# Weights split into two parts by two GpSimd-queue DMAs and a ScalarE negation, in a four-layer block on one Trainium2 core

## The chip, the core and the metric

The kernel runs on one core of one Trainium2 chip. The metric is device time in microseconds (us), as the median of three runs. The engines are TensorE (PE in the profile, PEld for its weight loads), VectorE (DVE), ScalarE (ACT), GpSimd (POOL) and SyncE (SP); SP, ACT and POOL can also issue DMAs, which all run on the core's 16 DMA engines.

## The reference

512 tokens of 1024 features in fp32 pass through four mixers with a residual each, and a norm at the end:

```
h = rms_norm(x) * (1 + scale) + shift          # scale, shift, gate = silu(c) @ ada_w[l] + ada_b[l]
x = x + gate * ([conv31(h @ Wa) | rwkv7(h @ Wb)] @ even_w_out)     # layer 0
x = x + gate * ((topk_attention(h @ odd_w_in) * silu(g)) @ odd_w_out)  # layer 1
x = x + (lru(conv4(h @ lru_w_in)) * gelu(gate)) @ lru_w_out         # layer 2, width 1536
x = x + (forgetting_attention(h @ fox_w) * silu(g)) @ fox_w_out     # layer 3, 16 heads of 64
out = rms_norm(x, final_g)
```

What matters here: every `@` with a weight matrix is an fp32 product, and the result is compared at fp32 accuracy.

## The kernel before

Activations lie with the features in the partitions: eight tiles of 128 features by 512 tokens. TensorE takes operands of type fp32r, which carry fewer bits than fp32. So each fp32 operand is written as the sum of two fp32r tiles, a first part h and a remainder l, and each product is three matmuls (`mm3`, lines 161 to 165): first weight part times first activation part (L163), first weight part times the remainder of the activations (L164), and the remainder of the weights times the first activation part (L165).

Weights are used once, in column tiles of [128 partitions, up to 8 row tiles, 128], 512 KB each, 384 KB for `lru_w_out`, and 256 KB where a product is taken in halves. `wsplit` (line 126) prepares one of them:

- SP issues a DMA of the raw weights into a tile `wr` of a ring of three (L133);
- ScalarE casts each half of it to fp32r, `wh` (L138);
- GpSimd subtracts, `wl = wr - wh`, for each half (L139). `wh` and `wl` are rings of four half tiles, that is two whole weight tiles.

`wrows` (line 143) does the same for the first eight loads, which hold one row tile of seven column tiles each: DMA L148, cast L153, subtraction L154. Callers are `project`, `fill`, `lead`, `project_halves` and `project_tok`; the last passes a tag (`pT`) for the last weights of the kernel, so that these stand in another ring.

Each engine runs its own instructions in order. The order is set when the kernel is built: a list scheduler places the instructions of all engines by its own model, with priorities, and tiles are handed out from rings, so that an instruction waits until the last user of its buffer is done. A DMA is issued by its queue's engine in that same order: what stands behind a waiting instruction waits too.

Other work that the prediction names: the convolution's 27 multiply-adds for each of eight channel tiles on DVE (L835), with L840 on POOL; the recurrence's L622, L626 and L628; the softmax scaling by rows on POOL (L1235, L1487); and L1088, two DMAs that POOL issues, of 64 partitions by 512 fp32 from SBUF to SBUF.

## Time and profile before

| | |
|---|---|
| runs | 1833.74, 1839.56, 1842.38 us; median 1839.56 |
| profiled execution, first to last instruction | 1835.4 us (no device time of its own is given for it) |
| PE | 1685.5 us busy, 92% |
| DVE | 1319.1 us busy, 72% |
| ACT | 899.9 us busy, 49% |
| POOL | 866.9 us busy, 47% |
| granted TensorE clock, mean | 0.955 |
| DMA | 182.15 MB, mean 99 GB/s |

The page gives busy time by engine, the chain of work that ended last, and groups of instructions by line. A matmul's busy time in it overlaps that of the next, so a busy PE is not a PE at its peak; the distance between the starts of two matmuls is the better measure. Waits are put down to what released them last.

### The profile page before, as it was taken

What the parts mean: (1) busy time and instruction counts of PE and PEld (TensorE: products, weight loads), DVE (VectorE), ACT (ScalarE), POOL (GpSimd) and SP (SyncE); (2) the same over time, 40 slices, a digit from 0 to 9 for tenths busy, and PEclk for the clock granted to TensorE, in tenths of its full rate; (3) what the DMA queues carried; (4) which work ended last, traced back from release to release, by engine and by line L of the source; (5) the groups of instructions that cost most, each with busy time, mean ns of one, the idle gap of its engine ahead of it and who ended that gap; (6) DMA issues with size and microseconds to landing.
All of it is one profiled execution on the core that took longest, in us unless ns stands there. A gap on an engine that the chain in (4) does not pass through costs nothing.

```text
span 1835.4 us, 25614 instructions
## 1 busy us (share of the span) xinstructions
PE 1685.5 (92%) x9250; PEld 1311.0 (71%) x9250; DVE 1319.1 (72%) x2246; ACT 899.9 (49%) x1699; POOL 866.9 (47%) x682
## 2 busy tenths in 40 slices
PE   3997889999895999898999999999988899999998
PEld 2765678776664777765778788888766687776776
DVE  6689997897969786568969978734898721455552
ACT  2443234334333524466344677644767633555564
POOL 4555564444585422354435555344544443444343
PEclk9997898998988889999999999999999999999999
DMA  9412352214243852331225310022222233321211
GB/s 271 131 58 69 118 144 72 83 47 135 78 126 120 266 185 97 97 99 58 92 86 169 119 53 13 24 92 92 81 89 66 78 103 108 104 81 61 81 55 70
DMA packets 111055, 182.15 MB, mean 99 GB/s; under 512 B 37296, under 2 KB 57136, under 8 KB 110928
## 3 DMA queue, kind: packets, MB, share of 16 engines
q1 hardware_dynamic: 106736, 172.91, 30.1%
q10 hardware_dynamic: 4032, 7.34, 1.1%
q8 instruction: 73, 1.20, 0.3%
q14 instruction: 54, 0.44, 0.1%
q0 software_dynamic: 160, 0.26, 0.1%
HBM read 162.10 MB, written 18.12 MB: 98 GB/s over the span
## 4 chain that ended last, share of the span: by engine, by line
PE 58%; DVE 32%; ACT 4%; issue 4%; DMA 2%; SPq 0%; POOL 0%; DVEq 0%; ACTq 0%
PE ps L163 15%; PE ps L164 15%; PE ps L165 14%; DVE x L835 7%; DVE q L665 2%; DVE xc L1300 2%; DVE q L666 2%; PE ps L1494 1%; DVE SAV L438 1%; DVE u L1369 1%; PE ps L706 1%; PE ps L1477 1%; PE ps L1490 1%; PE ps L1238 1%; PE ps L538 1%
## 5 line engine op out<-in xcount | busy, mean ns | idle before, releaser
L139 POOL TENSOR_TENSOR wl<-wr,wh 128x512 fp32r<-128x512 f32 (+1 forms) x400 | 563.6, 1413 | 657.1 <-ACT wh L138 614.3
L163 PE MATMUL ps<-h,wh 128*128 128x512 f32 x1240 | 511.2, 416 | 31.2 <-DVE s L516 13.2
L165 PE MATMUL ps<-h,wl 128*128 128x512 f32 x1240 | 505.7, 408 | 6.0 <-POOL wl L139 6.0
L164 PE MATMUL ps<-h,wh 128*128 128x512 f32 x1240 | 506.2, 408 | 3.2 <-DVE h L328 2.7
L138 ACT CAST wh<-wr 128x512 fp32r<-128x512 f32 (+1 forms) x400 | 242.0, 609 | 409.4 <-PE ps L164 332.4
L163 PEld LDWEIGHTS ps<-h,wh 128*128 128x128 f32 x1240 | 244.5, 197 | 98.8 <-DVE s L516 17.0
L165 PEld LDWEIGHTS ps<-h,wl 128*128 128x128 f32 x1240 | 243.5, 196 | 63.0 <-POOL wl L139 7.1
L164 PEld LDWEIGHTS ps<-h,wh 128*128 128x128 f32 x1240 | 244.0, 197 | 57.2 <-issue 3.6
L835 DVE SCALAR_TENSOR_TENSOR x<-cu,vec,x 128x512 f32<-128x512 f32 x216 | 214.5, 995 | 4.7
L1235 POOL TENSOR_SCALAR pp<-pp,st 128x512 f32<-128x512 f32 x32 | 52.3, 1634 | 51.9 <-DVE st L1231 38.3
L1484 DVE CUSTOM_DVE_ANT_0 pp<-ps,nb 128x128 f32<-128x128 f32 (+3 forms) x64 | 30.8, 488 | 42.4 <-PE ps L1479 31.2
L1230 ACT ACTIVATE pp<-pp,st 128x512 f32<-128x512 f32 x64 | 46.3, 723 | 23.8 <-DVE st L1229 23.6
L665 DVE TENSOR_TENSOR q<-q,q 128x112 f32<-128x112 f32 (+25 forms) x108 | 46.1, 461 | 15.0 <-POOL q L657 11.7
L1487 POOL TENSOR_SCALAR pp<-pp,st 128x128 f32<-128x128 f32 (+1 forms) x32 | 31.4, 986 | 47.9 <-DVE st L1486 47.8
L1229 DVE CUSTOM_DVE_ANT_0 pp<-ps,bias 128x512 f32<-128x512 f32 x64 | 43.4, 679 | 6.2 <-PE ps L1238 4.2
L164 PE MATMUL ps<-wl,h 128*128 128x512 f32 x120 | 47.2, 393 | 0.0
L1485 ACT ACTIVATE pp<-pp,st 128x128 f32<-128x128 f32 (+3 forms) x64 | 35.9, 561 | 21.8 <-DVE st L1484 21.3
L163 PE MATMUL ps<-wh,h 128*128 128x512 f32 x120 | 46.5, 403 | 0.0
L165 PE MATMUL ps<-wh,h 128*128 128x512 f32 x120 | 46.5, 393 | 0.0
L1491 ACT COPY pT<-ps 128x128 f32<-128x128 f32 (+3 forms) x64 | 26.6, 423 | 39.6 <-PE ps L1490 38.8
L284 DVE TENSOR_TENSOR pT<-ps,pT 128x512 fp32r<-128x512 f32 x64 | 43.4, 680 | 2.3 <-ACT pT L283 2.1
L283 ACT CAST pT<-ps 128x512 fp32r<-128x512 f32 x64 | 36.6, 577 | 16.2 <-PE ps L1238 15.7
(522 smaller groups left out, 3480.7 us busy)
## 6 DMA issues: line engine op xcount, KB each, us to landing
wr<-in_even_w_in SPq DMA_DIRECT2D x50, 512.0 KB, 3.5
wr<-in_odd_w_in SPq DMA_DIRECT2D x39, 512.0 KB, 3.5
wr<-in_lru_w_in SPq DMA_DIRECT2D x24, 512.0 KB, 3.4
wr<-in_fox_w_qkg SPq DMA_DIRECT2D x24, 512.0 KB, 3.5
k<-in_ada_w SPq DMA_DIRECT2D x32, 256.0 KB, 3.0
wr<-in_odd_w_out SPq DMA_DIRECT2D x16, 512.0 KB, 3.8
wr<-in_lru_w_out SPq DMA_DIRECT2D x16, 384.0 KB, 3.1
AR<-in_ada_w SPq DMA_DIRECT2D x4, 1024.0 KB, 9.8
```

The costliest lines, as they stand in the source:

```text
L138: nc.scalar.copy(h[:, :n], raw[:, k:k + n])
L139: nc.gpsimd.tensor_tensor(out=l[:, :n], in0=raw[:, k:k + n], in1=h[:, :n].bitcast(F), op=OP.subtract)
L163: mm(ps, lhsT=w[0], rhs=x[0], start=first, stop=False)
L164: mm(ps, lhsT=w[0], rhs=x[1], start=False, stop=False)
L165: self.last_mm = mm(ps, lhsT=w[1], rhs=x[0], start=False, stop=last).ins
L284: nc.vector.tensor_tensor(out=l, in0=src, in1=h.bitcast(F), op=OP.subtract)
L665: eng.tensor_tensor(out=z, in0=Yu[:, a, b:b + 1].to_broadcast(sh), in1=Nu[:, b:b + 1, b + 1:].to_broadcast(sh), op=OP.mult)
L666: eng.tensor_tensor(out=Yu[:, a, b + 1:], in0=Yu[:, a, b + 1:], in1=z, op=OP.add)
L835: nc.vector.scalar_tensor_tensor(out=acc, in0=u[:, q:q + S], scalar=w[q], in1=acc, op0=OP.mult, op1=OP.add)
L1229: nc.vector.tensor_tensor_reduce(out=pp, in0=lg, in1=bias[t], scale=1.0, scalar=3e38, op0=OP.add, op1=OP.min, accum_out=mx)
L1230: nc.scalar.activation(pp, pp, AF.Exp, scale=-1.0, bias=mx, accum_out=sm)
L1235: (nc.vector if t % 2 else nc.gpsimd).tensor_scalar(out=pp, in0=pp, scalar1=sm, scalar2=None, op0=OP.mult)
```

## The change

A new helper `wparts` takes the place of load, cast and subtraction. A DMA issued by POOL writes the weights into the fp32r tile `h`, rounding on the way; ScalarE writes `l = -h`; a second POOL DMA reads the same weights from HBM again and adds them to `l` in place. There is no `wr` ring any more; `wh` and `wl` become rings of three whole tiles. (Comments and docstrings are dropped too, so lines move up by up to four: L1088 becomes L1084.)

```diff
     def wsplit(self, key, idx, k0, kn, rows=True, tag=None):
...
-        raw = self.wp.tile([P, 8, P], F, name=self.name("wr"), tag="wr", bufs=3)
-        nc.sync.dma_start(out=raw[:, :kn], in_=self.ins[key][idx][:, k0:k0 + kn])
-        out = []
-        n = kn if kn <= 4 else kn // 2
-        for k in range(0, kn, n):
-            h, l = (self.t(tag, (P, 4, P), R) if tag else self.wp.tile([P, 4, P], R, name=self.name(z), tag=z, bufs=4) for z in ("wh", "wl"))
-            nc.scalar.copy(h[:, :n], raw[:, k:k + n])
-            nc.gpsimd.tensor_tensor(out=l[:, :n], in0=raw[:, k:k + n], in1=h[:, :n].bitcast(F), op=OP.subtract)
...
+        h, l = self.wparts(self.ins[key][idx][:, k0:k0 + kn], kn, tag)
...
+    def wparts(self, src, n, tag=None):
+
+        nc = self.nc
+        h, l = ((self.t(tag, (P, 8, P), R) if tag else self.wp.tile([P, 8, P], R, name=self.name(z), tag=z, bufs=3))[:, :n] for z in ("wh", "wl"))
+        nc.gpsimd.dma_start(out=h, in_=src)
+        nc.scalar.mul(l, h.bitcast(F), -1.0)
+        nc.gpsimd.dma_start(out=l, in_=src, accum_op=OP.add)
+        return h, l
 
     def wrows(self, key, ct, k):
...
-        nc.sync.dma_start(out=raw[:, :n], in_=self.ins[key][ct[0]:ct[-1] + 1:d, :, k].rearrange("c p n -> p c n"))
...
+        h, l = self.wparts(self.ins[key][ct[0]:ct[-1] + 1:d, :, k].rearrange("c p n -> p c n"), n)
+        return [(h[:, i], l[:, i]) for i in range(n)]
```

In the built program POOL then issues 217 first-part DMAs (L142) and 217 adding DMAs (L144), ScalarE 217 negations (L143), and SP none of the weight loads. In POOL's order, 159 of the 217 pairs have no other first-part DMA between their two; for 59 pairs the two follow each other directly. The names are tiles: `wh` and `wl` the two parts, `wr` the raw weights, `in_...` a weight matrix in HBM, `pp` a block of softmax numerators, `V` values by tokens.

POOL, the values' projection at the start of the last layer, before:

```order
L139 TENSOR_TENSOR wl_13447<-wr_13444,wh_13446 128x512
L139 TENSOR_TENSOR wl_13451<-wr_13444,wh_13450 128x512
L139 TENSOR_TENSOR wl_13516<-wr_13513,wh_13515 128x512
L139 TENSOR_TENSOR wl_13520<-wr_13513,wh_13519 128x512
L139 TENSOR_TENSOR wl_13550<-wr_13547,wh_13549 128x512
L139 TENSOR_TENSOR wl_13554<-wr_13547,wh_13553 128x512
```

and the same place as changed:

```order
L142 DMA wh_12608<-in_fox_w_v 128x1024
L144 DMA wl_12609<-in_fox_w_v 128x1024
L142 DMA wh_12672<-in_fox_w_v 128x1024
L144 DMA wl_12673<-in_fox_w_v 128x1024
L142 DMA wh_12701<-in_fox_w_v 128x1024
L144 DMA wl_12702<-in_fox_w_v 128x1024
```

Six subtractions became three pairs of DMAs; the load of a weight tile now stands behind the adding DMA of the tile before it.

ACT at that place, before:

```order
L138 CAST wh_13446<-wr_13444 128x512
L138 CAST wh_13450<-wr_13444 128x512
L1408 COPY rb_13320<-ps_13407 128x512
L138 CAST wh_13515<-wr_13513 128x512
L138 CAST wh_13519<-wr_13513 128x512
L1401 ACTIVATE V_13316<-ps_13321,col_13368 128x512
```

and as changed:

```order
L143 ACTIVATE wl_12609<-wh_12608 128x1024
L1404 COPY rb_12499<-ps_12576 128x512
L143 ACTIVATE wl_12673<-wh_12672 128x1024
L1397 ACTIVATE V_12495<-ps_12500,col_12542 128x512
L1397 ACTIVATE V_12496<-ps_12501,col_12542 128x512
L143 ACTIVATE wl_12702<-wh_12701 128x1024
```

Two casts became one negation of twice the size, which stands ahead of the same evacuations of PSUM and waits for a DMA that POOL issues.

POOL in the attention of layer 1, as changed; the scalings L1231 (L1235 before) now stand among the DMA pairs:

```order
L142 DMA wh_9557<-in_odd_w_in 128x1024
L1231 TENSOR_SCALAR pp_8264<-pp_8264,st_8266 128x512
L144 DMA wl_9558<-in_odd_w_in 128x1024
L142 DMA wh_9703<-in_odd_w_in 128x1024
L1231 TENSOR_SCALAR pp_8302<-pp_8302,st_8304 128x512
L1060 TENSOR_TENSOR s_8915<-s_8915,tab_6271 128x512
L144 DMA wl_9704<-in_odd_w_in 128x1024
L1231 TENSOR_SCALAR pp_8379<-pp_8379,st_8381 128x512
```

A scaling behind an L144 waits until that DMA has been issued.

## Rows read from the trace of the kernel before

**Rows 1.** The page, the chain that ended last: shares of the span by engine, by line.

```profile
PE 58%; DVE 32%; ACT 4%; issue 4%; DMA 2%; SPq 0%; POOL 0%; DVEq 0%; ACTq 0%
PE ps L163 15%; PE ps L164 15%; PE ps L165 14%; DVE x L835 7%; DVE q L665 2%; DVE xc L1300 2%; DVE q L666 2%; PE ps L1494 1%; DVE SAV L438 1%; DVE u L1369 1%; PE ps L706 1%; PE ps L1477 1%; PE ps L1490 1%; PE ps L1238 1%; PE ps L538 1%
```

**Rows 2.** The page's costliest groups: busy us, mean ns, idle before, releaser.

```profile
L139 POOL TENSOR_TENSOR wl<-wr,wh 128x512 fp32r<-128x512 f32 (+1 forms) x400 | 563.6, 1413 | 657.1 <-ACT wh L138 614.3
L138 ACT CAST wh<-wr 128x512 fp32r<-128x512 f32 (+1 forms) x400 | 242.0, 609 | 409.4 <-PE ps L164 332.4
L835 DVE SCALAR_TENSOR_TENSOR x<-cu,vec,x 128x512 f32<-128x512 f32 x216 | 214.5, 995 | 4.7
```

**Rows 3.** Timeline of PE at full pace: start, us, engine, line, operation.

```profile
98.54 0.39 PE L163 MATMUL ps<-h,wh 128*128 128x512 f32 x1
...
99.22 0.39 PE L163 MATMUL ps<-h,wh 128*128 128x512 f32 x1
```

**Rows 4.** Line 835 (DVE): duration in ns, min/median/max, first and last start.

```profile
L835 DVE SCALAR_TENSOR_TENSOR x<-cu,vec,x x216: 721/752/1826, 83.0 to 516.6; 128x512 f32<-128x512 f32 x108
```

**Rows 5.** Timeline of DVE and of POOL around 178 us.

```profile
178.48 1.83 DVE L835 SCALAR_TENSOR_TENSOR x<-cu,vec,x 128x512 f32<-128x512 f32 x1
180.83 0.74 DVE L628 SCALAR_TENSOR_TENSOR s<-s,vec,s 128x512 f32<-128x512 f32 x1
...
178.47 1.29 POOL L139 TENSOR_TENSOR wl<-wr,wh 128x512 fp32r<-128x512 f32 x1 [0.46 <-ACT wh L138]
```

**Rows 6.** The chain in order of time: first and last of its stretched DVE pieces.

```profile
21.09 1.65 DVE SAV L438
...
1449.77 1.93 DVE u L1369
```

**Rows 7.** The page's DMA issues: count, KB each, median us from issue to landing.

```profile
wr<-in_odd_w_in SPq DMA_DIRECT2D x39, 512.0 KB, 3.5
wr<-in_lru_w_out SPq DMA_DIRECT2D x16, 384.0 KB, 3.1
AR<-in_ada_w SPq DMA_DIRECT2D x4, 1024.0 KB, 9.8
wr<-in_even_w_out SPq DMA_DIRECT2D x16, 256.0 KB, 2.7
```

**Rows 8.** Line 1088, POOL's own DMAs: issue ns min/median/max; landing.

```profile
L1088 POOL DMA_DIRECT2D ki<-ki x2: 517/632/747, 805.7 to 806.9; - x2
DMA to landing us min/median/max: 2.2/2.3/2.4
```

**Rows 9.** Timeline of ACT around 96 us: a weight tile's two casts, merged.

```profile
96.29 1.13 ACT L138 CAST wh<-wr 128x512 fp32r<-128x512 f32 x2
```

**Rows 10.** Line 133, the weight loads by matrix: issue ns, first and last start.

```profile
L133 SPq DMA_DIRECT2D wr<-in_odd_w_in x39: 327/328/425, 760.4 to 1032.4; - x39
L133 SPq DMA_DIRECT2D wr<-in_lru_w_in x24: 327/328/328, 1238.1 to 1400.6; - x24
L133 SPq DMA_DIRECT2D wr<-in_fox_w_qkg x24: 327/328/384, 1532.5 to 1726.7; - x24
L133 SPq DMA_DIRECT2D wr<-in_lru_w_out x16: 327/328/328, 1408.2 to 1485.8; - x16
L133 SPq DMA_DIRECT2D wr<-in_fox_w_v x8: 327/328/375, 1490.0 to 1527.1; - x8
```

**Rows 11.** Line 148, the first eight loads: issue to landing.

```profile
DMA to landing us min/median/max: 4.7/6.6/11.0
```

**Rows 12.** The page's DMA queue of SP: packets, MB, share of 16 engines.

```profile
q1 hardware_dynamic: 106736, 172.91, 30.1%
```

**Rows 13.** Timeline of PE after an idle stretch.

```profile
107.14 0.63 PE L164 MATMUL ps<-h,wh 128*128 128x512 f32 x1
107.56 0.63 PE L165 MATMUL ps<-h,wl 128*128 128x512 f32 x1
```

More of the change, by code (lines that the diff above doesn't have):

```diff
@@ L131, in wsplit @@
         nc = self.nc
-        raw = self.wp.tile([P, 8, P], F, name=self.name("wr"), tag="wr", bufs=3)
-        nc.sync.dma_start(out=raw[:, :kn], in_=self.ins[key][idx][:, k0:k0 + kn])
-        out = []
-        n = kn if kn <= 4 else kn // 2
-        for k in range(0, kn, n):
-            h, l = (self.t(tag, (P, 4, P), R) if tag else self.wp.tile([P, 4, P], R, name=self.name(z), tag=z, bufs=4) for z in ("wh", "wl"))
-            nc.scalar.copy(h[:, :n], raw[:, k:k + n])
-            nc.gpsimd.tensor_tensor(out=l[:, :n], in0=raw[:, k:k + n], in1=h[:, :n].bitcast(F), op=OP.subtract)
-            out += [(h[:, i], l[:, i]) for i in range(n)] if rows else [[z.rearrange("p a c -> p (a c)") for z in (h, l)]]
-        return out
+        h, l = self.wparts(self.ins[key][idx][:, k0:k0 + kn], kn, tag)
+        if rows:
+            return [(h[:, i], l[:, i]) for i in range(kn)]
+        n = kn // 2
+        return [[z[:, k:k + n].rearrange("p a c -> p (a c)") for z in (h, l)] for k in (0, n)]
+    def wparts(self, src, n, tag=None):
[5 more added lines that the diff above has]
+        return h, l
     def wrows(self, key, ct, k):
         nc = self.nc
-        raw = self.wp.tile([P, 8, P], F, name=self.name("wr"), tag="wr", bufs=3)
         n, d = len(ct), ct[1] - ct[0]
-        nc.sync.dma_start(out=raw[:, :n], in_=self.ins[key][ct[0]:ct[-1] + 1:d, :, k].rearrange("c p n -> p c n"))
-        out = []
-        for o in (0, 4):
-            m = min(4, n - o)
-            h, l = (self.wp.tile([P, 4, P], R, name=self.name(z), tag=z, bufs=4) for z in ("wh", "wl"))
-            nc.scalar.copy(h[:, :m], raw[:, o:o + m])
-            nc.gpsimd.tensor_tensor(out=l[:, :m], in0=raw[:, o:o + m], in1=h[:, :m].bitcast(F), op=OP.subtract)
-            out += [(h[:, i], l[:, i]) for i in range(m)]
-        return out
+        h, l = self.wparts(self.ins[key][ct[0]:ct[-1] + 1:d, :, k].rearrange("c p n -> p c n"), n)
+        return [(h[:, i], l[:, i]) for i in range(n)]
     def prefetch(self, key, idx, k0=0, kn=8):
```

## The prediction

> **What bounds the kernel now.** I read the chain of waits first: TensorE holds 58% of it and VectorE 32%, GpSimd and SP nothing [rows 1]. So GpSimd's subtraction of the weights, 563.6 us of work, is hidden as work; what it waits for is ScalarE's cast, and the cast waits for TensorE to free a buffer [rows 2]. Weights are ready before they are wanted. TensorE's own pace is in the timeline: the three matmuls of a row tile take 99.22 - 98.54 = 0.68 us [rows 3], so a weight tile of eight row tiles is used up in 8 x 0.68 = 5.45 us. That is the number a new way of feeding has to meet.
>
> The second thing to see is that GpSimd's work is not free for VectorE. The same multiply-add L835 takes 752 ns at the median, but 995 on average and up to 1826 [rows 2, 4]. The timeline says when: one that runs beside a subtraction L139 takes 1.83 us, while a multiply-add with no GpSimd work beside it takes 0.74 [rows 5]. In the chain in order of time, the 195 longest pieces hold 89 single VectorE instructions of 1.6 to 1.9 us [rows 6]; set against GpSimd's instructions, 63 of them run beside an L139 above all. So part of VectorE's 32% is L139's doing.
>
> **The change part by part.**
>
> *GpSimd's subtractions go.* 63 pieces, each longer by some 0.95 us (1.7 less 0.75), are 60 us on the chain. GpSimd's other instructions stay and stretch some of the same places, and behind a shortened piece the next wait is near, mostly TensorE's. Bounds: 0 and -60; I take three quarters, **-45 us**. It counts in layers 0 and 2, where these pieces lie.
>
> *SP's 217 loads and ScalarE's casts go, ScalarE's negations come.* SP is not on the chain; nothing gained. Two casts of half a tile take 1.13 us together [rows 9]; a negation of the whole tile should take about the same. Nothing.
>
> *The feed now turns on GpSimd's queue.* For one weight tile GpSimd issues the first-part DMA, which must land; ScalarE negates; only then GpSimd can issue the adding DMA, and in 159 of 217 pairs no other first-part DMA is issued meanwhile. So a tile costs GpSimd's queue a cycle: landing + negation + issue of the adding DMA.
> - Landing of the first part: SP's plain load of 512 KB lands in 3.5 us, 256 KB in 2.7 [rows 7], so 0.8 us for 256 KB and 1.6 us for a tile's own bytes. GpSimd's two DMAs of before land in 2.2 to 2.4 us for 128 KB [rows 8], no later than SP's trend. The next first part is issued right behind an adding DMA of at least as many bytes in the same queue, so I take 3.5 + 1.6 = 5.1. What rounding costs no row shows. Bounds: 3.5, and 9.8, which 1024 KB take [rows 7].
> - Negation: 1.13.
> - Issue: 0.63 us for 64 partitions [rows 8]; for 128 between 0.63 and twice that, 1.26. I take 0.95.
>
> The cycle is 5.1 + 1.13 + 0.95 = 7.2 us, with bounds 5.3 and 12.2. It is longer than TensorE's 5.45. For the 384 KB tiles it is (3.1 + 1.2) + 0.85 + 0.95 = 6.1 [rows 7].
>
> What that costs is read by stage from the loads of before [rows 10]. The values' projection takes a tile each 37.1 / 7 = 5.3 us: 8 x (7.2 - 5.3) = 15. `lru_w_out`: one each 77.6 / 15 = 5.2, so 16 x (6.1 - 5.2) = 15. `odd_w_in` and `lru_w_in` take one each 7.2 and 7.1 us on average: 0 and 3 if their three buffers level out every burst. That is 33 us as a floor. If no burst is levelled out, their 63 tiles at full pace lose 7.2 - 5.45 each, 110, so 140 as a ceiling. The other stages take one in over 8 us (the gates and queries: 194.2 / 23 = 8.4) and hide it. I take the middle, **+87 us**.
>
> The second bound, the ring: a slot is held from the issue of the first part to TensorE's last use, 7.2 + some 5 for the adding DMA + 5.45, and three slots make that 5.9 us per tile, under the cycle. It costs nothing while the cycle is 7.2.
>
> *The first eight loads* land in 6.6 us [rows 11]; their cycle is 6.6 + 1.0 + 0.95 = 8.5 against 7 x 0.68 = 4.8 of TensorE. Only three fit ahead; the five others cost between 0 (TensorE waits for other things there) and 5 x 3.7 = 18. I take **+10**.
>
> *What stands behind the wait.* GpSimd stands still up to 6 us in a pair. Behind it are the softmax scalings L1235 and L1487, 32 each, whose results TensorE transposes, and the recurrence's products. Half of 64 delayed by 3 us each would be about 96; four buffers of `pp` lie between, and some pairs have the scaling between their DMAs. Bounds 0 and 96; I take a fifth, **+20**. ScalarE's negation likewise holds up the evacuations behind it, but no longer waits for TensorE itself, which cost it 332 us off the chain [rows 2]; I set these against each other.
>
> *DMA engines.* SP's 172.91 MB took 30.1% of the 16 engines [rows 12]. Reading 107 MB of weights a second time adds 19 points, and reading the tile to be added to as much again: about 70%, not a bound by itself.
>
> **The sum:** -45 + 87 + 10 + 20 = +72, so 1835.4 + 72 = 1907 us from first to last instruction. The median of the runs lies 4.2 us above that span, so **1912 us**, +3.9% on 1839.56. About 0.5% is what a measurement of this kernel can tell from no change.
>
> One amplifier: after an idle stretch TensorE's matmuls start 0.42 us apart [rows 13] instead of 0.23, the lower of its two levels, 1.2 GHz. New waits in layers 1 to 3, where the clock now is nearly all at full, would pay that on top; it is in the upper end.
>
> **The rivals.**
>
> *Faster: the cycle fits.* If the first part lands in 3.5 us and an issue takes 0.63, the cycle is 5.3, under 5.45, and neither feed nor start costs anything; the relief of VectorE remains: 1835 - 45 + 4 = 1795. For it: GpSimd's DMAs of before land as fast as SP's. Against: the queue, which puts each first part behind an adding DMA. It decides at a cycle of about 6 us, where loss and gain cancel. Chance 0.27.
>
> *No change:* the two cancel within 0.5%, 1840. Chance 0.10.
>
> *Much slower: rounding or adding runs at a lower rate.* With a cycle of 10 us (the first part lands in about 8, towards the 9.8 of 1024 KB) the stages lose, levelled out, 39 x 10 - 272 = 118, 78, 16 x 8.5 - 78 = 58, 43 and 46 us (`odd_w_in`, `lru_w_in`, `lru_w_out`, values, queries and gates), together 343; with the 63 tiles at full pace 287 in place of 118 + 78, together 434; the middle is 389. With the other terms 1835 + 389 - 45 + 30 + 4 = 2213. For it: no row shows such a DMA. Against: nothing but that SP's rows show no rate so low. Chance 0.17.
>
> *Slower: the adding DMA moves its tile twice.* If it moves 2 x 512 KB, 3.2 us, the first part behind it lands in up to 6.7 us and the cycle is 8.8. The same reckoning gives 178 as a floor and 283 as a ceiling, 230 in the middle, and 1835 + 230 - 45 + 30 + 4 = 2054. It decides where first part and adding DMA follow each other at once. Chance 0.10. The Trainium skill states such a rule in "Collectives: The Full Stack", Part 3: an add inside a DMA costs no time of its own but needs two source reads, and so runs at half the rate of a copy; no run here shows it.
>
> *Slower: GpSimd's issue is held up by VectorE.* The two engines get in each other's way [rows 5]; if each issue waits for a VectorE instruction of 0.7 us, twice per tile, the cycle is 8.6, and the time about 2035 by the same reckoning. L1088's two issues, 517 and 747 ns [rows 8], tell little. Chance 0.05. The Trainium skill has the rule in "SBUF — State Buffer", "Who interferes with whom": while VectorE runs in a two-port mode, GpSimd cannot write its DMAs' descriptors.
>
> The forecast's own case, a cycle of 6.3 to 8, keeps 0.31.
>
> **How the numbers follow.** Faster: 0.27 and a little of the forecast's lower edge, 0.28. Same: 0.10. Slower: the rest, 0.62. The likeliest case by itself runs from 1850 to 1990. The range takes in the fast case, down to a relief of 55 us (1785), the two cases between, and most of the low-rate case (up to 2220), so **1785 to 2220**; what is left out is a cycle above 10 and a relief above 55.
>
> **What would show it.** Right: GpSimd's waits before the adding DMAs (L144) take most of its time and end on ScalarE's negation; ScalarE's negations end on DMAs; TensorE's waits before L163 and L165 in the values' projection and in `lru_w_out` end on GpSimd's DMAs; tiles there come every 7 us. L835's mean falls towards 752 ns. Wrong: L835 stays near 995 (no relief); first parts land in 3.5 us and TensorE does not wait for weights (the fast case); first parts land in 8 us or more (the low-rate case); or the stages lose nothing and time goes in the attention instead, behind scalings that come late.

## The result, and the profile after

The changed kernel takes 2006.59 us (median of 4 runs, 2001.93 to 2007.98), the kernel before beside it 1836.94: **9.2% slower**, ratio 1.0919 [1.0892, 1.0946]. The forecast was 1912: its direction was right, and 2006.59 lies in the range, but the loss is +170 us where +72 was forecast. The profiled execution took 2005.2 us, at a mean granted clock of 0.932 (0.955 before). One correction to what stands ahead: layer 2's gate is silu, not gelu; nothing rests on it.

The page of the changed kernel, the chain that ended last:

```profile
PE 32%; issue 27%; DMA 13%; DVE 11%; POOL 7%; ACT 2%; SPq 0%; POOLq 0%; DVEq 0%; ACTq 0%
PE ps L161 7%; PE ps L159 7%; PE ps L160 7%; POOL wl L144 3%; POOL wh L142 3%; DMA wl<-in_even_w_in 2%; DMA adm<-in_ada_w 2%; DVE x L831 1%; DMA k<-in_ada_w 1%; DMA wh<-in_odd_w_in 1%; PE ps L1490 1%; PE ps L702 1%; DMA wl<-in_lru_w_in 1%; PE ps L1473 1%; DVE q L662 1%
```

VectorE falls from 32% of the chain [rows 1] to 11%. GpSimd's two DMA lines and the weights' landings, absent before, are now in it. "Issue" stands for time that no wait in the profile explains; it rises from 4% to 27%, and in the chain in order of time 452 of its 540 us stand directly before GpSimd's DMAs L142 and L144, so most of it is time of that queue too. Groups of the same page (busy us, mean ns | idle before, releaser):

```profile
L143 ACT ACTIVATE wl<-wh 128x1024 fp32r<-128x1024 f32 (+3 forms) x216 | 217.5, 1007 | 571.1 <-DMA wh<-in_even_w_in 151.8
L831 DVE SCALAR_TENSOR_TENSOR x<-cu,vec,x 128x512 f32<-128x512 f32 x216 | 179.6, 832 | 4.5
L1231 POOL TENSOR_SCALAR pp<-pp,st 128x512 f32<-128x512 f32 x32 | 52.5, 1642 | 68.9 <-DVE st L1227 60.7
L161 PE MATMUL ps<-y,wl 128*128 128x512 f32 x96 | 41.7, 436 | 21.5 <-DMA wl<-in_lru_w_out 21.5
```

The multiply-add, 995 ns on average before [rows 2], takes 832: the relief is there. ScalarE's negation waits for the first part's landing, as forecast. The idle time before the softmax scaling ends on VectorE (60.7 of 68.9 us); a delay behind an adding DMA would not show in that figure. In `lru_w_out` TensorE waits for the adding DMA.

GpSimd's waits (us in total, times, longest):

```profile
POOL wl L144 <- ACT wl L143: 715.0, 172, 9.6
POOL wh L142 <- PE ps L161: 342.8, 91, 14.5
```

The first is the cycle of the forecast. The second, a first part that waits until TensorE has freed a slot, is the ring, which the forecast put at nothing. The timeline of GpSimd in `odd_w_in` shows the cycle (start us, us; in brackets the idle time before):

```profile
902.55 0.85 POOL L144 DMA_DIRECT2D wl<-in_odd_w_in  x1 [6.75 <-ACT wl L143]
903.48 0.55 POOL L142 DMA_DIRECT2D wh<-in_odd_w_in  x1
906.06 1.72 POOL L1060 TENSOR_TENSOR s<-s,tab 128x512 f32<-128x512 f32 x1 [2.02 <-ACT s L1058]
910.96 0.86 POOL L144 DMA_DIRECT2D wl<-in_odd_w_in  x1 [3.18 <-ACT wl L143]
```

and ScalarE's negation in it:

```profile
909.60 1.06 ACT L143 ACTIVATE wl<-wh 128x1024 fp32r<-128x1024 f32 x1 [1.72 <-DMA wh<-in_odd_w_in]
```

From one adding DMA to the next are 910.96 - 902.55 = 8.4 us: the adding DMA's issue 0.85, the next first part's landing 6.1 (its own issue of 0.55 and 5.6 from then on; the page too counts a landing from the start of the issue), the negation 1.06, and 0.4 between them. The forecast had 7.2. Over the 23 tiles of `odd_w_in` whose pair stands alone, behind the adding DMA of the tile before, the median is 8.7 us. DMA issues of the page (count, KB, median us to landing) and the queues:

```profile
wh<-in_odd_w_in POOLq DMA_DIRECT2D x39, 512.0 KB, 5.8
wl<-in_odd_w_in POOLq DMA_DIRECT2D x39, 512.0 KB, 5.6
wh<-in_lru_w_in POOLq DMA_DIRECT2D x24, 512.0 KB, 6.0
...
k<-in_ada_w SPq DMA_DIRECT2D x32, 256.0 KB, 5.4
...
wh<-in_even_w_in POOLq DMA_DIRECT2D x8, 448.0 KB, 9.6
```

```profile
q0 software_dynamic: 74944, 214.20, 49.5%
q1 hardware_dynamic: 69344, 65.94, 11.3%
```

Where do the 170 us come in? The same VectorE, ScalarE and GpSimd instructions were matched between the two traces, and the shift of their starts (each trace from its own start) taken as the median over 25 us of the old time. In places it changes by 10 us from one such stretch to the next, so a stage's share is good to some 10 us. Beside it stand two experiments that come below: a fourth slot, and the kernel before without the subtraction.

| end of the stage, by the old time | shift after | with a fourth slot | without the subtraction |
|---|---|---|---|
| start and first eight loads, 75 us | +25 | +8 | -5 |
| layer 0, input and convolution, 550 | +13 | -17 | -71 |
| `even_w_out`, 775 | +54 | +7 | -79 |
| `odd_w_in` and attention, 1175 | +84 | +20 | -95 |
| `odd_w_out`, 1300 | +115 | +28 | -100 |
| layer 2's recurrence, 1400 | +121 | +14 | -116 |
| `lru_w_out`, 1475 | +142 | +15 | -121 |
| values' projection, 1550 | +163 | +15 | -121 |
| end, 1825 | +170 | +21 | -122 |

### The profile page after: what moved, and what is told of

It is laid out like the page before. It is cut to its first block, busy times and chain, and to the rows that moved or that the text cites. A ratio compares the mean times of both kernels' runs of the same rounds, so it can differ in the third digit from the quotient of the medians.

```text
span 2005.2 us, 25137 instructions
## 1 busy us (share of the span) xinstructions
PE 1748.6 (87%) x9250; PEld 1346.7 (67%) x9250; DVE 1144.0 (57%) x2246; ACT 872.4 (44%) x1500; POOL 599.1 (30%) x698
## 3 DMA queue, kind: packets, MB, share of 16 engines
q0 software_dynamic: 74944, 214.20, 49.5%
## 4 chain that ended last, share of the span: by engine, by line
PE 32%; issue 27%; DMA 13%; DVE 11%; POOL 7%; ACT 2%; SPq 0%; POOLq 0%; DVEq 0%; ACTq 0%
PE ps L161 7%; PE ps L159 7%; PE ps L160 7%; POOL wl L144 3%; POOL wh L142 3%; DMA wl<-in_even_w_in 2%; DMA adm<-in_ada_w 2%; DVE x L831 1%; DMA k<-in_ada_w 1%; DMA wh<-in_odd_w_in 1%; PE ps L1490 1%; PE ps L702 1%; DMA wl<-in_lru_w_in 1%; PE ps L1473 1%; DVE q L662 1%
## 5 line engine op out<-in xcount | busy, mean ns | idle before, releaser
L143 ACT ACTIVATE wl<-wh 128x1024 fp32r<-128x1024 f32 (+3 forms) x216 | 217.5, 1007 | 571.1 <-DMA wh<-in_even_w_in 151.8
L831 DVE SCALAR_TENSOR_TENSOR x<-cu,vec,x 128x512 f32<-128x512 f32 x216 | 179.6, 832 | 4.5
L144 POOL DMA_DIRECT2D wl<-in_even_w_in x58 | 58.1, 1001 | 159.3 <-ACT wl L143 155.2
L144 POOL DMA_DIRECT2D wl<-in_odd_w_in x39 | 34.1, 875 | 148.6 <-ACT wl L143 142.7
L142 POOL DMA_DIRECT2D wh<-in_even_w_in x58 | 41.4, 728 | 118.8 <-PE ps L161 112.0
L1231 POOL TENSOR_SCALAR pp<-pp,st 128x512 f32<-128x512 f32 x32 | 52.5, 1642 | 68.9 <-DVE st L1227 60.7
L161 PE MATMUL ps<-y,wl 128*128 128x512 f32 x96 | 41.7, 436 | 21.5 <-DMA wl<-in_lru_w_out 21.5
L144 POOL DMA_DIRECT2D wl<-in_fox_w_qkg x24 | 20.9, 871 | 128.7 <-ACT wl L143 120.9
L1226 ACT ACTIVATE pp<-pp,st 128x512 f32<-128x512 f32 x64 | 46.1, 720 | 13.0 <-DVE st L1225 12.6
L144 POOL DMA_DIRECT2D wl<-in_lru_w_in x24 | 20.8, 865 | 95.6 <-ACT wl L143 90.3
L142 POOL DMA_DIRECT2D wh<-in_even_w_out x24 | 14.0, 585 | 117.4 <-PE ps L161 97.1
L1156 DVE SCALAR_TENSOR_TENSOR acc<-rl,wi,acc 128x512 f32<-128x512 f32 x32 | 26.0, 814 | 39.7 <-ACT rl L1155 39.3
```

The costliest lines, as they stand in the source:

```text
L142: nc.gpsimd.dma_start(out=h, in_=src)
L143: nc.scalar.mul(l, h.bitcast(F), -1.0)
L144: nc.gpsimd.dma_start(out=l, in_=src, accum_op=OP.add)
L161: self.last_mm = mm(ps, lhsT=w[1], rhs=x[0], start=False, stop=last).ins
L831: nc.vector.scalar_tensor_tensor(out=acc, in0=u[:, q:q + S], scalar=w[q], in1=acc, op0=OP.mult, op1=OP.add)
L1156: nc.vector.scalar_tensor_tensor(out=acc, in0=rl, scalar=ki["w"][:, 8 * t + h:8 * t + h + 1], in1=acc, op0=OP.mult, op1=OP.add)
```

## The experiments

Three theories went in: Q, the cycle of GpSimd's queue, one tile after the other; R, the ring of three slots; D, the load on the DMA engines by the second read.

**1. The first part a tile early, and a fourth slot for it.** The program keeps a list of all 217 tiles, so that each one can start the next one's first part; `wfirst(j)` takes a slot of `wh`, of which there are four, and issues the rounding DMA of tile j. The diff is cut to the lines that matter here.

```diff
-        nc.gpsimd.dma_start(out=h, in_=src)
...
+        for j in (i, i + 1):
+            if j not in self.firsts and j < len(SEQ) and (j == i or not SEQ[j][-1] == "pT"):
+                self.wfirst(j)
+        h = self.firsts[i]
...
         nc.scalar.mul(l, h.bitcast(F), -1.0)
         nc.gpsimd.dma_start(out=l, in_=src, accum_op=OP.add)
```

> The changed kernel, with one thing moved: GpSimd issues the first-part DMA of the next weight tile before the adding DMA of this one, so that the landing (5.3 us) no longer stands inside every cycle of its queue. Same DMAs, same bytes (289 MB). The ring of first parts has four slots in place of three, so that the earlier issue finds one free. Theory Q (GpSimd's queue works one tile after the other, 5.3 + 1.06 + 0.87 = 7.2 us each): most of the 170 us come back, 1840 to 1890 us. Theory D (the DMA engines carry too much): nothing changes, 1990 to 2020 us. Theory R (three slots of each part are too few because a slot is now held from the issue of the first part on): some of it comes back through the fourth slot of the first part, but the second part still has three, 1940 to 1990 us.

Measured: 1852.8 us, ratio 1.0084 [1.0067, 1.0101]. 154 of the 170 us come back with the same DMAs and bytes, so D is not the main cause. It looked like Q; the next run says that this was too early.

**2. The fourth slot alone.**

```diff
-        h, l = ((self.t(tag, (P, 8, P), R) if tag else self.wp.tile([P, 8, P], R, name=self.name(z), tag=z, bufs=3))[:, :n] for z in ("wh", "wl"))
+        h, l = ((self.t(tag, (P, 8, P), R) if tag else self.wp.tile([P, 8, P], R, name=self.name(z), tag=z, bufs=3 + (z == "wh")))[:, :n] for z in ("wh", "wl"))
```

> The changed kernel with four slots in place of three for the first parts; the second parts keep three, and the order of the DMAs on GpSimd's queue stays: adding DMA of this tile, then first part of the next. It tells how much of what the early first part gave back (2006 to 1853 us) was its fourth slot. Theory Q (the order in the queue is what costs): little, 1970 to 2010 us. Theory R (the slots cost): most of it, 1860 to 1910 us; in that case GpSimd's wait for freed first-part slots, 343 us in the changed kernel, shrinks to under 150.

Measured: 1860.17 us, 1.0139 [1.0104, 1.0174], nearly the same gain. By the expectation that is R; but the wait for first-part slots did not shrink, it grew from 343 us to 513, so R's own sign is missing:

```profile
POOL wh L142 <- PE ps L161: 513.0, 140, 16.7
```

The trace says why: the order changed as well. With three slots 159 of the 217 pairs have no other first part between their two DMAs, with four slots 1. The list scheduler places a first part when its model has a slot free, which is the likely reason: a fourth slot puts nearly every first part ahead of the adding DMA before it. GpSimd's timeline in `odd_w_in` of this run:

```profile
880.68 0.59 POOL L142 DMA_DIRECT2D wh<-in_odd_w_in  x1 [3.06 <-PE ps L161]
882.47 0.86 POOL L144 DMA_DIRECT2D wl<-in_odd_w_in  x1 [1.20 <-ACT wl L143]
883.54 1.29 POOL L1060 TENSOR_TENSOR s<-s,tab 128x512 f32<-128x512 f32 x1 [0.21 <-ACT s L1058]
886.12 0.60 POOL L142 DMA_DIRECT2D wh<-in_odd_w_in  x1 [1.29 <-PE ps L161]
887.91 0.86 POOL L144 DMA_DIRECT2D wl<-in_odd_w_in  x1 [1.19 <-ACT wl L143]
891.55 0.56 POOL L142 DMA_DIRECT2D wh<-in_odd_w_in  x1 [2.77 <-PE ps L161]
```

Here a tile takes 5.4 us from one first part to the next (886.12 - 880.68, 891.55 - 886.12), which is TensorE's pace of 5.45 [rows 3]. The landing is gone from between the two DMAs. GpSimd waits for TensorE: in this stretch the feed is ahead.

**3 and 4. Order and slots taken apart.** One run has three slots and the early order throughout; one has four slots and the late order throughout. In the first the adding DMA is tied behind the next first part, in the second each first part behind the adding DMA before it (`issue_after`).

```diff
-        nc.gpsimd.dma_start(out=l, in_=src, accum_op=OP.add)
+        with self.tc.issue_after(self.last_first):
+            nc.gpsimd.dma_start(out=l, in_=src, accum_op=OP.add)
```
```diff
-        nc.gpsimd.dma_start(out=h, in_=src)
+        with self.tc.issue_after(self.last_add) if self.last_add else contextlib.nullcontext():
+            nc.gpsimd.dma_start(out=h, in_=src)
...
-        nc.gpsimd.dma_start(out=l, in_=src, accum_op=OP.add)
+        self.last_add = nc.gpsimd.dma_start(out=l, in_=src, accum_op=OP.add).ins
```

> The changed kernel with three slots of each part, as it had, but GpSimd's queue put in the other order throughout: the first part of the next tile always ahead of the adding DMA of this one. The run with a fourth slot for the first parts turned out to have this order almost everywhere as well, because the order of the queue is planned from what is free; so slot and order went together until now. Theory Q (the order costs: landing, negation and issue of one tile after the other, 8.4 us per tile where the pair stands alone): 1860 to 1890 us. Theory R (the slots cost): 2000 us or more, since an early first part now waits for a slot in front of the adding DMA that TensorE needs.

> The run with four slots for the first parts and three for the second, but GpSimd's queue kept in the late order throughout: the first part of a tile only behind the adding DMA of the tile before it. Theory Q: every tile now pays the cycle of 7.2 to 8.4 us, and the fourth slot stands empty; 2000 to 2060 us. Theory R: the fourth slot helps as it did, 1860 to 1890 us.

Measured: 2013.61 us (1.0933 [1.0881, 1.0985]) and 2104.56 us (1.1467 [1.1422, 1.1511]). The second is even slower than the 2060 us that Q allowed. Neither helps alone; both theories were half right. GpSimd with the early order and three slots:

```profile
886.05 0.55 POOL L370 DMA_DIRECT2D wh<-in_odd_w_in  x1 [7.85 <-PE ps L400]
886.59 0.92 POOL L383 DMA_DIRECT2D wl<-in_odd_w_in  x1
...
893.26 0.59 POOL L370 DMA_DIRECT2D wh<-in_odd_w_in  x1 [3.46 <-PE ps L400]
893.84 0.94 POOL L383 DMA_DIRECT2D wl<-in_odd_w_in  x1
...
900.48 0.59 POOL L370 DMA_DIRECT2D wh<-in_odd_w_in  x1 [4.38 <-PE ps L400]
```

GpSimd waits before a first part (L370 here) in 161 cases until L400, TensorE's last matmul with a tile, frees a slot, and the adding DMA (L383), whose negation is long done, stands behind it. In this stretch that makes 7.2 us per tile.

```profile
POOL wh L370 <- PE ps L400: 847.9, 161, 17.0
```

With the late order and four slots (L144 the first part, L146 the adding DMA):

```profile
964.72 0.85 POOL L144 DMA_DIRECT2D wh<-in_odd_w_in  x1
972.61 0.88 POOL L146 DMA_DIRECT2D wl<-in_odd_w_in  x1 [7.04 <-ACT wl L145]
973.17 0.88 POOL L144 DMA_DIRECT2D wh<-in_odd_w_in  x1
981.25 0.87 POOL L146 DMA_DIRECT2D wl<-in_odd_w_in  x1 [7.20 <-ACT wl L145]
```

No wait for a slot, and the bare cycle: 981.25 - 972.61 = 8.6 us per tile. So it takes an early order to be rid of the cycle, and a spare slot to make the early order free. The changed kernel has a mixture of the two bad cases (159 of its 217 pairs late, and three slots), and comes out near the first of them.

**5. Two plain DMAs.** The wait inside the pair is taken away.

```diff
-        nc.scalar.mul(l, h.bitcast(F), -1.0)
-        nc.gpsimd.dma_start(out=l, in_=src, accum_op=OP.add)
+        nc.gpsimd.dma_start(out=l, in_=src)
```

> The changed kernel without the negation, and with a plain rounding DMA in place of the adding one, so that the second part is a second copy of the first: the remainder of the weights is left out of the result. GpSimd issues two DMAs per tile that wait for nothing but free slots; 0.6 + 0.6 us of its queue. The bytes read from HBM stay 289 MB; what adding reads of the tile itself goes. Theory Q: the wait inside the cycle is gone, 1800 to 1840 us, less than before the change because VectorE runs beside no subtraction. Theory D: two loads of every weight remain, 1950 to 2010 us. Theory R: a slot is held 2 to 4 us less, some of it comes back, 1900 to 1960 us.

Measured: 1762.55 us, 0.9592 [0.9567, 0.9616], below the ranges of all three theories. Every weight is still read twice from HBM, with three slots, through the same queue. What is left of the loss against this run, 2006.6 - 1762.6 = 244 us, hangs on the chain landing, negation, adding, with the slots that it holds. The run also takes work from the DMA engines, since it adds nothing:

```profile
q0 software_dynamic: 74944, 214.20, 38.9%
```

where the changed kernel has 49.5%. That D is not the main cause rests on run 1 too, which keeps every adding DMA.

**6. No subtraction.** The kernel before, with `l = h` and GpSimd's subtraction left out.

> The kernel before, with GpSimd's subtraction left out: the second part is the first part again, so the remainder of the weights is left out of the result. It measures by itself what VectorE gains when GpSimd does not work beside it, the term that the prediction put at -45 us with bounds 0 and -60. By that term: 1790 us (1777 to 1837). By the run with two plain DMAs, which came 74 us below the kernel before: 1760 to 1775 us, then the relief is larger than the upper bound. Without any wait of TensorE for the subtraction in the kernel before, nothing else should move.

Measured: 1721.53 us, 0.9373 [0.9339, 0.9407], so -116 us, nearly twice the upper bound of the forecast's relief, and below the 1760 to 1775 that run 5 had suggested. The group of the multiply-add on its page:

```profile
L835 DVE SCALAR_TENSOR_TENSOR x<-cu,vec,x 128x512 f32<-128x512 f32 x216 | 177.9, 826 | 4.4
```

The multiply-adds lose 214.5 - 177.9 = 37 us; all of VectorE falls from 1319.1 us busy to 1127.6, so four fifths of that fall lie in other lines, from 17 us downward each (L665 falls from 46.1 to 29.5). The clock rises from 0.955 to 0.981. The run also takes away the subtraction's own time between cast and matmul, so it is an upper size of the relief, not VectorE's share to the last us. That part is small: in the kernel before TensorE waited some 6 us in all for the subtraction.

```profile
L165 PE MATMUL ps<-h,wl 128*128 128x512 f32 x1240 | 505.7, 408 | 6.0 <-POOL wl L139 6.0
```

It and the run before split the change into steps: 1836.9 - 116 (no subtraction) + 41 (two DMAs per tile, no wait between) + 244 (the wait between, the adding, and slots) = 2006. These are differences of measured times, so the sum comes out by itself; it is no check.

**7. The first load by SP**, into a ring of three raw tiles; `wh` and `wl` are rings of two whole tiles each (their lines are left out of the diff).

```diff
-        nc.gpsimd.dma_start(out=h, in_=src)
-        nc.scalar.mul(l, h.bitcast(F), -1.0)
+        nc.sync.dma_start(out=raw, in_=src)
+        nc.scalar.copy(h, raw)
+        nc.scalar.mul(l, raw, -1.0)
         nc.gpsimd.dma_start(out=l, in_=src, accum_op=OP.add)
```

> The changed kernel with the first load taken from GpSimd's queue: SP loads the raw weights into a ring of three tiles, ScalarE casts them to the first part and writes their negative, and GpSimd only issues the DMA that adds the raw weights from HBM. Bytes as in the changed kernel, 289 MB; the rings of first and second parts have two whole tiles each, as before the change. ScalarE does one more pass of some 1.1 us for each tile. Theory Q: the landing leaves GpSimd's queue, which then holds 0.9 us of issue and a wait for ScalarE per tile; 1820 to 1870 us. Theory D: the same bytes cost the same, 1980 to 2020 us. Theory R: with two slots of each part it becomes worse than the changed kernel or stays, 2000 us and more.

Measured: 2130.16 us, 1.1608 [1.1572, 1.1644]. Q's 1820 to 1870 failed: the landing had left GpSimd's queue, and the time rose. The waits name the ring:

```profile
POOL wl L146 <- ACT wl L145: 1024.8, 158, 17.2
ACT wh L144 <- PE ps L162: 305.9, 90, 11.9
```

GpSimd waits for the negation, the cast before it for a slot that TensorE frees (another 291 us before the cast end on nothing that the profile shows). By estimate a slot is held for cast and negation 2.0, issue 1.0, landing 7.7 and use 5.45, 16 us; two slots make that 8 us per tile, and 8.05 is the median distance of the adding DMAs in `odd_w_in`. It was the first sign that slots are not free.

**8. The second load by itself.** The kernel before, with a second transfer of each raw tile but the first eight into a scratch tile in HBM.

> The kernel before, with a second transfer of each weight tile from HBM that nobody waits for (SP issues it, into a scratch tile in HBM). It adds 107 MB of reads, and as many written, to the DMA engines and leaves the feed of the weights as it was. Theory D: the ada loads, the spilled tiles and the weights come late, 1920 us and more, +85 or more of the 170. Theories Q and R: little, 1840 to 1870 us.

Measured: 2139.52 us, 1.1636 [1.1612, 1.166]. The experiment missed its aim: nothing holds these transfers back, so all of them were issued in the first 369 us. Two stretches (us, then PE, PEld, DVE, ACT, POOL busy; clock, DMA share, GB/s):

```profile
0.00:375.00 375.00, 65.60 (x218) 50.61 (x218) 72.83 (x107) 29.18 (x48) 34.71 (x34) 0.62 0.98 320
375.00:2140.00 1765.00, 1637.04 (x9032) 1272.60 (x9032) 1241.81 (x2139) 869.91 (x1652) 824.57 (x649) 0.95 0.29 94
```

The engines were 98% busy for 375 us, and the whole 305 us were lost there; it says nothing of the stages behind. Runs 11 and 12 put the question better.

**9. Half tiles.** The changed kernel with all DMAs, negations and slots of 256 KB, eight half slots of `wh` and six of `wl`: the memory of four and three whole ones.

> The changed kernel in half tiles: each DMA, negation and slot holds 256 KB, with eight half slots for the first parts and six for the second (the memory of four and three whole ones). A slot comes free twice as often, and a landing takes some 3.3 us in place of 5.3, but GpSimd issues four DMAs per tile, 2 x (0.6 + 0.87) = 2.9 us. Theory Q: the order is early nearly everywhere again, 1840 to 1870 us. Theory R: finer slots are worth more than whole ones, 1800 to 1840 us. If issuing is what counts (four DMAs per tile): 1880 us and more.

Measured: 1825.16 us, 0.9932 [0.9908, 0.9955]: inside the 1800 to 1840 us that R gave, and 35 us below whole slots (run 2), though GpSimd issues four DMAs per tile.

**10. Early first parts in some layers only.** The kernel before; in layer 0's input projection (and in a second run in layer 2's too) the three slots of the raw weights take first parts, issued early, and the second parts are made in halves in the rings of `wh` and `wl`.

> The kernel before in all stages but one: in layer 0's input projection, from its ninth tile on (50 tiles), the first part comes by a rounding DMA of GpSimd's queue, issued one tile early, ScalarE negates it in two halves, and two adding DMAs of 256 KB finish the second part; the slots of the raw weights hold the first parts there. Tiles are wanted there every 8 to 9 us or slower, so the cycle of 7 to 8 us should be hidden, and VectorE loses the subtractions beside it. Theory Q: 1800 to 1825 us, faster than both kernels (the early first part was 19 us ahead of the kernel before at the end of this stage). Rival: three slots for first parts hold up the adding DMAs here too, and the gain is lost, 1835 to 1870 us.

> As the run with layer 0 alone, and the 24 tiles of layer 2's input projection the same way. The early first part gained 20 us on the kernel before between the start of that stage's recurrence and its end, after losing a few at its beginning. Theory Q: 1785 to 1815 us, 10 to 20 us below the run with layer 0 alone. Rival: the 12 tiles at full pace at the stage's start cost what the rest gives, and it stands within 5 us of that run.

Measured: 1833.09 us, 0.9968 [0.9946, 0.9991], and 1853.36 us, 1.0091 [1.0063, 1.0119]. The first fell between its two forecasts. The second rose where a gain of 10 to 20 was expected: layer 2 lost 23 us with three slots for first parts, where the run with four had gained 14 from 1300 to 1400 us (table). That points to the slots again, but the second parts come in halves here as well, so it does not show it.

**11. Adding from SBUF, in halves.** This takes the first part off GpSimd's queue as run 7 does, but in the rings of the kernel before, four half slots each.

```diff
             nc.scalar.copy(h[:, :n], raw[:, k:k + n])
-            nc.gpsimd.tensor_tensor(out=l[:, :n], in0=raw[:, k:k + n], in1=h[:, :n].bitcast(F), op=OP.subtract)
+            nc.scalar.mul(l[:, :n], h[:, :n].bitcast(F), -1.0)
+            nc.gpsimd.dma_start(out=l[:, :n], in_=raw[:, k:k + n], accum_op=OP.add)
```

> The kernel before, rings and half tiles as they are, with GpSimd's subtraction alone replaced: ScalarE writes the negative of the first part, and GpSimd issues a DMA that adds the raw weights from their slot in SBUF. No weight is read from HBM a second time, the first part does not wait for GpSimd at all, and VectorE loses the subtractions beside it. ScalarE gets one more pass of 0.55 us per half, GpSimd 0.87 us of issue. Theory Q: GpSimd's queue holds no landing, so this is faster than both kernels, 1760 to 1810 us. Theory R: a slot of the second part is held some 5 us longer than before (negation, issue, landing) with four half slots, (0.5 + 0.5 + 0.9 + 4 + 2.7) / 4 = 2.2 us per half against 2.7 of TensorE, so it just holds: 1780 to 1850 us. If the DMA's landing in SBUF is 6 us and more, the ring is the bound and it is 1900 us or more.

Measured: 1813.39 us, 0.988 [0.9834, 0.9925], faster than both kernels, 3 us above what Q gave and inside R's range. Its adding DMAs, and the queue that holds nothing else of size:

```profile
wl<-wr POOLq DMA_DIRECT2D x376, 256.0 KB, 4.3
q0 software_dynamic: 60352, 107.24, 35.3%
```

**12. The same, adding from HBM** (`in_=` the weights in place of `raw`).

> As the run that adds the raw weights from their slot in SBUF (1813 us), but the adding DMA reads them from HBM a second time, as the changed kernel does. Everything else is the same, so the difference is the price of the second read from HBM. Theory D (the second read of 107 MB, and what it does to the other transfers, is a large part of the 170 us): 1880 us and more. Theories Q and R: within 15 us, 1800 to 1830 us; a raw slot even comes free earlier.

Measured: 1834.06 us, 0.9984 [0.9966, 1.0002]. The second read costs 1834.1 - 1813.4 = 21 us here, a little above the 15 that Q and R allowed. That is D's size, where the engines carry much at any rate: an eighth of the change's 170, if it is the same there.

**13 and 14. Adding only where it pays.** The run with SBUF adding gave up 37 us of its lead in `even_w_out`. One run keeps GpSimd's subtraction there; the other adds only in layer 0's input projection and layer 2's two projections.

```diff
-            nc.gpsimd.tensor_tensor(out=l[:, :n], in0=raw[:, k:k + n], in1=h[:, :n].bitcast(F), op=OP.subtract)
+            if not key.startswith(("even_w_in", "lru_w")):
+                nc.gpsimd.tensor_tensor(out=l[:, :n], in0=raw[:, k:k + n], in1=h[:, :n].bitcast(F), op=OP.subtract)
+            else:
+                nc.scalar.mul(l[:, :n], h[:, :n].bitcast(F), -1.0)
+                nc.gpsimd.dma_start(out=l[:, :n], in_=raw[:, k:k + n], accum_op=OP.add)
```

> As the run that adds from SBUF, with GpSimd's subtraction kept in layer 0's output projection (24 tiles), where that run lost 37 us of its lead again: DMA engines are busiest there and VectorE's ada products wait for their loads. If the loss there is the adding DMAs' traffic, it comes back: 1780 to 1800 us, faster than both kernels. Rival: the loss is VectorE's own work catching up (the lead at the stage's start was slack), then 1805 to 1820 us.

> As the run that adds from SBUF, but only in layer 0's input projection and layer 2's projections, where VectorE's row of multiply-adds runs beside the subtraction; everywhere else GpSimd subtracts as before. If VectorE is held up by the subtraction only there, the leads of those stages stay (30 to 34 us at the end of layer 0's input, some 17 in layer 2) and nothing is lost elsewhere: 1785 to 1800 us. Rival: the subtraction costs in the attention layers too (the run without any subtraction gained 20 us there), and it stands above 1805 us.

Measured: 1800.74 us, 0.9793 [0.9766, 0.982], and **1796.48 us, 0.9779 [0.9757, 0.9802]**: 2.2% below the kernel before. The two are the fastest of those that make both parts of the weights in full, and too close to be told apart. In the second the shift stands at -28 at 550 us, stays at -31 from 800 to 1250, and ends at -40, so the relief that this way gives lies in layers 0 and 2, as the forecast said (run 6 gained 16 us in layer 1 too).

The first run's expectation put the loss in `even_w_out` down to the traffic of the adding DMAs. The lead does stay with the subtraction there (-28 at 600 us, -27 at 750, where run 11 goes from -29 to -10). But run 12, whose second read adds traffic, keeps its lead in that stage as well (-26 to -20). What run 11 has and run 12 has not is that a raw slot is held until the adding DMA has read it. Whether that is the reason was not tested.

## Why the prediction was right in direction and wrong in size

**The step that failed** is the price of nothing for the ring and for most stages: "It costs nothing while the cycle is 7.2" and "The other stages take one in over 8 us ... and hide it". By the table the stages that had a price came to 30 + 6 + 21 + 21 = 78 us (`odd_w_in` with the attention, layer 2's input, `lru_w_out`, values) against the 87 forecast. The rest is outside them: +41 us in `even_w_out`, +31 in `odd_w_out`, +25 at the start (10 forecast), +7 at the end, and a gain of only 12 in layer 0's input. With the 78 this is the 170. In run 3 nearly every first part is issued early, so that the landing is out of the cycle; GpSimd waits for slots instead, and the loss is the same, 176 us. How the changed kernel's 170 divide between ring and cycle stays open, since both act in one queue.

The total is also nearer than its parts. Against run 6 the feed costs 2006.6 - 1721.5 = 285 us where 87 + 10 + 20 = 117 were forecast, and the relief is up to 116 where 45 were. Two errors in opposite directions partly cancel: that is luck.

**The bound and the mechanism: right.** The feed turned on GpSimd's queue, at a cycle of landing, negation and issue longer than TensorE's 5.45 us; TensorE waited for landings in the values' projection and in `lru_w_out`. Run 4 shows the bare cycle, runs 1 and 2 what is left when the landing is out of it. GpSimd's waits before the adding DMAs are its longest, 715 us, though not most of its time. Tiles came every 7.2 us in the values' projection (1645.1 to 1695.7 us for eight first parts, 50.6 / 7), the number forecast, but by chance: the second and third, issued early, come 4.6 and 5.3 us after the one before, the others 7.0 to 9.9.

**The cycle's size: a term too small.** "I take 3.5 + 1.6 = 5.1" and "Issue: 0.63 ... I take 0.95" gave 7.2 us; the trace shows 8.4. What was too small is the landing: 5.7 to 6.2 us in `odd_w_in`, `lru_w_in`, the values, and the queries and gates, counted from the start of the issue as in [rows 7], and 6.1 in the cycle shown. Pauses of 0.4 us come on top. The adding DMA's issue (0.87) lies well inside the bounds, and the negation, 1.06, was right. With 8.4 in the same reckoning, the stages of the floor lose 39 x (8.4 - 7.2) = 47 us in `odd_w_in` and 24 x (8.4 - 7.1) = 31 in `lru_w_in` in place of 0 and 3: next to a stage's mean, a cycle of 7.2 costs nothing and one of 8.4 costs 78. The miss is not there, though: the two stages came in at 36, below the 57 or so that the middle gave them; 15 of their 63 pairs are not late, and VectorE's relief counts in them too.

**Why the landing was late: a rival's mechanism.** The forecast counted the adding DMA as one more transfer of the tile's bytes. The rival that had it move the tile twice gave a landing of up to 6.7, a cycle of 8.8 and 2054 us, 47 us from the result where the forecast is 95 off; the cycle is borne out, while the total has the same stages at nothing or little. The queue's engine time shows the adding: GpSimd's DMAs took 38.9% of 1766.8 us = 687 us in the run with two plain DMAs, 49.5% of 2005.2 = 993 here. If a plain pass is 344, the adding pass is 649, 1.9 times as much for the same bytes written. Run 7, where the queue holds the adding DMAs alone, has 29.3% of 2128.1 = 624.

```profile
q0 software_dynamic: 37552, 107.23, 29.3%
```

The Trainium skill's rule in "Collectives: The Full Stack", Part 3, that an add in a DMA reads two sources and runs at half a copy's rate, agrees with the 1.9. The adding shows in the landings too, once one takes the DMAs that were issued when everything before them in the queue had landed (512 KB, stages behind layer 0's): ten first parts took 3.8 us at the median, 78 adding DMAs 5.5. The rounding one is 0.3 above SP's 3.5 [rows 7], which rules out a low rate of rounding. The 55 first parts issued within 0.5 us of an adding DMA took 6.45, which is 2.6 more than alone, where the forecast allowed 1.6. In run 4, where every first part follows an adding DMA, the median is 6.3.

**The rival of the held-up issue.** Its 2035 us is the number nearest to the result, but its mechanism is not there. It asked for 0.7 us more per issue, 304 us over the 434; they took 347 us in all, 50 more than if each had been as short as the shortest of its kind (0.53 and 0.84 us).

**A slip in the low-rate rival.** "39 x 10 - 272" takes the time of 38 distances between loads from that of 39 tiles, and so do the terms beside it; by the mean distances its floor is some 30 us lower. Nothing rests on it.

**"It costs nothing while the cycle is 7.2": wrong.** The ring was reckoned by an average hold over three slots, and next to the cycle, as if the longer of the two counted. Both stand in one queue: a first part that waits for a slot also holds the adding DMA behind it (run 3). And the number of slots set the order in which the scheduler laid the queue, 159 late pairs or 1. The fourth slot was worth 2006.6 - 1860.2 = 146 us.

**"The other stages take one in over 8 us ... and hide it": wrong.** A stage's mean does not show that it hides the cycle. `even_w_out` cost 54 - 13 = 41 us and `odd_w_out` 115 - 84 = 31, at 9.0 and 12.5 us per tile on average before (by their first and last loads). In `odd_w_out` order and slots act together again: the stage costs 8 us in run 2, but 41 and 45 in runs 3 and 4. In `even_w_out` the fourth slot leaves 24 us (table), and GpSimd waits long for slots; in the changed kernel:

```profile
755.76 0.56 POOL L142 DMA_DIRECT2D wh<-in_even_w_out  x1 [8.54 <-PE ps L161]
759.70 0.88 POOL L144 DMA_DIRECT2D wl<-in_even_w_out  x1 [3.37 <-ACT wl L143]
775.12 0.55 POOL L142 DMA_DIRECT2D wh<-in_even_w_out  x1 [14.54 <-PE ps L161]
```

It waits up to 14.5 us for a slot. Sixteen tiles of that stage hold 256 KB and still take a whole slot each, but finer slots did not help: the half slots of run 9 lose some 30 us there. Two plain DMAs with the same three slots lose nothing (run 5), so the loss hangs on negation and adding; how is open.

**The relief: right in kind, sized too low.** -45 with a bound of -60 was read from the 63 longest pieces on the chain, all taken as beside L139; without the subtraction the kernel gains 116. The shortest of the 195 pieces read is 1.2 us, so stretched instructions below that were not among them. In the changed kernel VectorE is as free (1144.0 us busy against 1127.6), yet layer 0 keeps only 25 - 13 = 12 us of the 66 that the run without subtraction shows there: the feed takes the rest.

**The start: +25, not +10.** The first eight land in 9.6 us, not the 6.6 of SP's loads [rows 11]. Most of the loss is the ring again: with a fourth slot the shift is +8 (table), though the landings still take 8.2 us there.

**The softmax scalings: +20 forecast, nothing seen.** The shift is flat through the later part of layer 1's attention (85 at 1075 us, 84 at 1175), where 20 of the 32 scalings run, and from 1575 us to the end of layer 3 it grows by 4 us. The first 12, from 965 us on, lie where the shift still grows with `odd_w_in`, and a delay by them cannot be told from the feed's there.

**DMA engines: a real but smaller term.** "Not a bound by itself" holds for the whole (62% over the span where about 70 were forecast), but loads beside it do suffer (the ada loads take 5.4 us for 3.0 before), and run 12 prices the second read at 21 us.

**The clock.** The mean granted clock fell from 0.955 to 0.932, as the forecast's amplifier has it; what that alone costs was not taken apart.

## What to carry to other kernels

When a producer needs two DMAs of one in-order queue with a wait between them, write down the whole cycle, every issue in it too, and look at the order in which the pairs are laid: a lookahead of one tile takes the landing out of the cycle, but only with a slot to spare, since a first part that waits for a slot blocks the step that TensorE wants. Do not take a stage's mean distance between tiles as proof that the cycle is hidden, and price the ring in the same queue as the cycle, not beside it. An engine's work can also be dear where it only slows another: taking the whole subtraction away shows the upper size of that, and moving it in the two layers where it hurts gave 2.2%.

## What the runs showed of the hardware that was not expected

- Adding DMAs took 1.8 to 1.9 times the engine time of rounding ones with the same bytes written (624 and 649 us against 344 for 107 MB), from HBM; from SBUF the adding ones took 35.3% of 1806.8 = 638 us for the same 107 MB. Reading the added operand from SBUF does not make it land much earlier either: 256 KB in 4.3 us, against 4.7 to 5.1 from HBM.
- With nothing of its queue ahead of it, a rounding DMA of 512 KB landed in 3.8 us, near SP's plain 3.5 [rows 7], and an adding one in 5.5 (changed kernel, medians of 10 and 78).
- What two DMAs of one queue take depends on their order: a first part lands in 4.6 us and its adding DMA in 7.9 with the early order (run 3, `odd_w_in`), in 6.5 and 5.5 with the late one (run 4). The sum hardly moves; which of the two the engines wait for does.
- Reads from HBM written back to HBM held the 16 engines at 98% with 320 GB/s (run 8, its first 375 us), and first weights landed in 14.0 us in place of 6.6.
